# Layer 0 of a two-layer decoder trunk: a finer program order, and one set of tiles for the inverses of two heads

## The chip, the cores and the metric

The kernel runs on 1 core of one Trainium2 chip. The metric is the device time of an execution in microseconds, as the median of the runs. TensorE is called PE here (its weight loads PEld), VectorE DVE, ScalarE ACT, GpSimd POOL, and the queue that issues nearly all DMAs is SyncE's, SP.

## What is computed

Two layers of a decoder on 256 tokens of width 1024, fp32. Layer 0 mixes tokens with Gated DeltaNet (8 heads of 128), layer 1 with sparse attention; both layers also attend to 256 memory tokens with 4 heads, and both end in a gated convolutional feed-forward (width 2816). The part that matters here is Gated DeltaNet for one head, in chunks of the sequence (the kernel uses two chunks of 128 tokens, the reference four of 64; the result is the same):

```
L = where(strict, (k*beta) @ k.T * decay, 0)
T = inverse(I + L)                       # unit lower triangular
u = T @ (v*beta);  w = T @ (k*beta*exp(gc))
a = where(incl, q @ k.T * decay, 0)
for each chunk n:
    v_new = u_n - w_n @ state
    o_n   = (q_n*exp(gc)) @ state + a_n @ v_new
    state = state * g_last + (k_n*exp(gc_last - gc)).T @ v_new
out = rms_norm(o) * silu(z)
```

## The kernel before

**An order made by a planner.** The program is not issued as written. Each call on an engine is recorded as an operation with the tiles that it reads and writes (`Eng`, from line 393), and `Sched.order` then places the operations one by one, as a list scheduler: of the operations that are ready on each engine it takes the one that can start first by the plan's own clock, and among those that could start at once the one that comes first in the program (`op.prio`). It looks at most 1500 operations past the first one not yet placed (`WINDOW`). Buffers of a ring are given out in program order. So the order of the program is an order of priorities. `Sched._cost` gives the duration that the plan assumes for an operation; for a matmul in fp32 with n columns and m output rows it was `(0.009 if m > 32 else -0.028) + 4 * max(m, n) / 2400`, which is 0.0253 us for 32 by 32. Operations made under `PE.group()` or `A.group()` are placed as one. The engines then run what they were given in that order, each in its own.

**Products in halves.** Weights come in chunks of 128x1024 fp32 through SP (`Weights`); ACT rounds a chunk to a high part (`wh`), DVE subtracts for the low part (`wl`), and PE does three products for each block of 128 rows (`proj`: high by high, high by low, low by high, of 256 columns). Tiles of such products are called `pj` (projections of layer 0 and 1) and `pf` (memory keys and values); other PSUM tiles are `mx`.

**Layer 0.** `gdn_pair(p)` is a generator for two heads; `next` runs it to its next `yield`. Before, it has three parts: (A) for both heads, projections of q, k, v, the short convolution, transposes, L (`LL`) and the masked q k product (`AT`); (B) the inverse of I + L for both heads; (C) the projection of z for both, and for both heads the two chunks of state, output and norm. Part B writes LL to DRAM (`scl`) and reads back its 16x16 diagonal blocks, one on each partition (`Lb`); DVE and POOL invert these in 15 steps of two operations (`tm`, `DD`; the planner chooses the engine of each); the result goes to DRAM (`scd`) and comes back laid out by rows (`cd`). Then the blocks are merged on PE: from 16 to 32 rows on the four 32-row quarters of the array (`quads`), from 32 to 64, and from 64 to 128, in two products each (`LL` by the inverse, then the inverse by that), with copies by ACT and DVE between them. Before, these merges run for each head in tiles of its own: `D32` (four buffers), `X`, two PSUM tiles for each step, and the inverse itself in one of four fixed tiles `full`.

The program order of layer 0 was: the memory keys of heads 1 to 3; then by the string `dd0dddddd01021321323`, where `d` is the decay of one head (a DMA, two selects on POOL, four exponentials on ACT) and a digit is the next part of that pair; then the memory values, then the four memory queries with their attention, then `out_proj`. Behind it come the memory keys and values of layer 1 and the feed-forward.

Of the kernel before, what the change touches and what calls it, by code (L numbers as in the profile page):

```python
# [19 lines left out]
P = 128  # L20
# [372 lines left out]
class Eng:  # L393
# [6 lines left out]
    def __getattr__(self, m):  # L400
        def call(*a, **kw):
            op = self._g or Op(self._e)
            op.calls.append((m, a, kw))
            op.name = op.name or m
            args = list(a) + list(kw.values())
            also_out = kw.pop("also_out", ())
            for t in kw.pop("also_in", ()):
                op.reads.add(t)
            outs = ([kw["out"]] if "out" in kw else [a[0]]) + list(also_out)
            if "accum_out" in kw:  # L410
                outs.append(kw["accum_out"])
            for x in args + list(also_out):
                if isinstance(x, (Vt, Ap)):
                    t = x.t if isinstance(x, Ap) else x
                    if t.base is None and t.cls == "whole":
                        continue
                    (op.writes if any(x is o for o in outs) else op.reads).add(t)
            c = self._cost(m, a, kw, outs[0], self._e)
            kw.pop("runs", None)
            op.cost += c  # L420
            if self._o:
                op.alt = {e: (op.alt or {}).get(e, 0.0) + self._cost(m, a, kw, outs[0], e) for e in self._o}
            op.dma = m == "dma_start"
            if m == "activation" and a[2] in (AF.Exp, AF.Silu):
                op.table = a[2]
            if self._g is None:
                self._s.add(op)
            return op
        return call

    def _cost(self, m, a, kw, out, e):
# [6 lines left out]
        if e == "tensor":  # L438
            n = math.prod(out.shape[1:])
            rhs = a[2]  # L440
            if m == "transpose":
                return 0.11
            dt = (rhs.t if isinstance(rhs, Ap) else rhs).dt
            m = out.shape[0]
            if dt == F32R:
                return max(0.013 + 2 * m / 2400, 0.01 + n / 2290)
            return (0.009 if m > 32 else -0.028) + 4 * max(m, n) / 2400
        if e == "vector":
            if m == "reciprocal":
                return 0.06 + 0.0065 * n  # L450
# [29 lines left out]
class Weights:  # L480
# [24 lines left out]
    def block(self, b, n=1):  # L505
# [3 lines left out]
        hi, lo = self.ready[c]  # L509
        return hi[:, r * P:(r + n) * P], lo[:, r * P:(r + n) * P]  # L510


CLASSES = {"q": 12, "d": 37, "k": 57, "s": 43, "ps": 8}

# [15 lines left out]
def body(ctx, tc, xT, memT, vecs, consts, rows, relb, w_few, w_in0, w_out0, w_up0, w_dn0, w_in1, w_out1, w_up1, w_dn1,  # L530
# [37 lines left out]
    def mx():  # L568
        return sc.tile("ps", [P, 512], F32, "mx", 6)
# [165 lines left out]
        kTm[layer, h] = K("kTm", 2 * MH)  # L735
        evac(ps, rm, kTm[layer, h])

    def mem_v(layer, ws, xs, rc):
        for p in range(MH // 2):
            ps = proj_t(ws, (MH + 2 * p) * KD, xs, "pf")  # L740
            for t in range(2):
                v = K("vm", 2 * MH)
                A.mul(v, ps[t], rc[:, t:t + 1])
                vm[layer, p, t] = v

    def mem_attn(layer, h, qmT, rcs=None):
        pss = mx()
# [228 lines left out]
            A.activation(g2[:, t], g2[:, t], AF.Exp, bias=gc[:, t, h:h + 1], scale=-1.0)  # L976
        decays.append((g1, g2))

    full = [fixed([P, 3, P], f"full{i}") for i in range(4)]
    for t in full:  # L980
        PO.memset(t, 0.0)

    def gdn_pair(p):
# [3 lines left out]
        for e, h in enumerate(hd):  # L987
# [47 lines left out]
                V.scalar_tensor_tensor(LL[e][:, t], pgm[:, t * S:t * S + P], sr[:, t:t + 1], g2[:, t], op0=OP.mult, op1=OP.mult)  # L1035
            for t in range(2):
                V.scalar_tensor_tensor(AT[e][:, t], pgm[:, t * S + P:(t + 1) * S], rr[:, t:t + 1], g1[:, t], op0=OP.mult, op1=OP.mult)

        yield

        sl = sc.tile("scl", [4 * US], F32, "scl", 2)
        for e in range(2):
# [9 lines left out]
        for k in range(IB - 1):  # L1052
# [11 lines left out]
        SY.dma_start(cd.rearrange("p w u i -> p (w u) i"),  # L1064
                    sd.raw(lambda r: bass.AP(tensor=r.tensor, offset=r.offset, ap=[[IB, P], [NB * IB * IB, 8], [1, IB]]),
                           [P, 8, IB]), runs=8 * P)

        bd = cst[:, C_BD - C_TRI:C_BD + 2 - C_TRI][:, None, :, None].to_broadcast([P, 2, 2, IB])
        quads = [slice(u, u + 32) for u in range(0, P, 32)]
        for e in range(2):  # L1070
            D = DX[e] = K("D32", 4, shape=(P, 2, 2, 32))
            for w in range(2):
                V.tensor_tensor(out=D[:, w].rearrange("p t (c i) -> p t c i", c=2),
                                in0=cd[:, w, 2 * e:2 * e + 2][:, :, None, :].to_broadcast([P, 2, 2, IB]), in1=bd, op=OP.mult)
            p1 = mx()
            with PE.group():
                for u in quads:
                    for t in range(2):
                        mm(p1[u, t * 32:(t + 1) * 32], LL[e][u, t, u], D[u, 1, t], start=True, stop=True)
            X = K("X", 3, shape=(P, 2, 32))  # L1080
            V.tensor_tensor(out=X, in0=two(p1[:, :64]), in1=D[:, 1], op=OP.add)
            p2 = mx()
            with PE.group():
                for u in quads:
                    for t in range(2):
                        mm(p2[u, t * 32:(t + 1) * 32], X[u, t], D[u, 0, t], start=True, stop=True)
                        mm(p2[u, 64 + t * 32:96 + t * 32], D[u, 0, t], X[u, t], start=True, stop=True)
            V.scalar_tensor_tensor(D.rearrange("p w t i -> p (w t i)"), D.rearrange("p w t i -> p (w t i)"), 2.0, p2[:, :P],
                                   op0=OP.mult, op1=OP.subtract)

        for e in range(2):
            D, F = DX[e], full[hd[e] % 4]
            for u in quads:
                A.copy(F[u, :2, u], D[u, 1])
            for u in quads[:2]:
                A.copy(F[u, 2].rearrange("p (t k) -> p t k", t=2)[:, :, u], D[u, 0])
            p1 = mx()
            with PE.group():
                for E, O in (quads[:2], quads[2:]):
                    for t in range(2):  # L1100
                        mm(p1[E, t * 32:(t + 1) * 32], LL[e][O, t, E], D[O, 1, t], start=True, stop=True)
            X = K("X", 3, shape=(P, 2, 32))
            with A.group():
                for E in quads[::2]:
                    A.copy(X[E], two(p1[E, :64]))
            p2 = mx()
            with PE.group():
                for E, O in (quads[:2], quads[2:]):
                    for t in range(2):
                        mm(p2[E, t * 32:(t + 1) * 32], D[E, 0, t], X[E, t], start=True, stop=True)  # L1110
                for t in range(2):
                    E, O = quads[:2]
                    mm(p2[O, t * 32:(t + 1) * 32], X[E, t], D[E, 0, t], start=True, stop=True)
            with A.group():
                for E, O in (quads[:2], quads[2:]):
                    A.mul(F[E, :2, O], two(p2[E, :64]), -1.0)
                E, O = quads[:2]
                A.mul(F[O, 2].rearrange("p (t k) -> p t k", t=2)[:, :, E], two(p2[O, :64]), -1.0)
        for e in range(2):
            F = DX[e] = full[hd[e] % 4]  # L1120
            E, O = slice(0, 64), slice(64, P)
            p1 = mx()
            with PE.group():
                for t in range(2):
                    mm(p1[E, t * 64:(t + 1) * 64], LL[e][O, t, E], F[O, t, O], start=True, stop=True)
            X = K("X", 3, shape=(64, 2, 64))
            A.copy(X, two(p1[E, :P]))
            p2 = mx()
            with PE.group():
                for t in range(2):  # L1130
                    mm(p2[E, t * 64:(t + 1) * 64], F[E, 2, t * 64:(t + 1) * 64], X[:, t], start=True, stop=True)
            A.mul(F[E, :2, O], two(p2[E, :P]), -1.0)

        yield

# [1 line left out]
        for e, h in enumerate(hd):  # L1137
            ps = proj(w0, (h * 4 + 3) * KD, hs)
            zs[e] = K("zs", 4)
            silu(zs[e], ps, ps, fastz)  # L1140
        for e, h in enumerate(hd):
            pu = mx()
            mm(pu[:, :P], DX[e][:, 0], bv[e][:, 0], start=True, stop=True)
# [36 lines left out]
            y = K("oz", 1)  # L1180
            V.scalar_tensor_tensor(y, pot[:, :S], (vecb if fastz else gnw)[:, 0:1], zs[e], op0=OP.mult, op1=OP.mult)
            mix[h] = hilo(y, "mix", 12, True)

    classes["scl"] = classes["scd"] = 2
    classes["gsc"] = 1
    pools["scl"] = pools["scd"] = pools["gsc"] = pools["dram"]
    for h in range(1, MH):
        mem_k(0, h, wm0, *ms0[:2])
    prs = [gdn_pair(p) for p in range(H // 2)]
    dh = 0  # L1190
    for ch in "dd0dddddd01021321323":
        if ch == "d":
            decay(dh)
            dh += 1
        else:
            next(prs[int(ch)], None)
    mem_v(0, wm0, ms0[0], ms0[2])
    b0 = 32 * KD
    for h in range(MH):
        ps = proj(w0, b0 + h * KD, hs)  # L1200
        q = K("qm", 2)
        A.copy(q, ps)
        mix[H + h] = mem_attn(0, h, q)
    out_proj(w_out0, mix[H:] + mix[:H])
    mts = []
    for k in range(0, KD, 2):
# [5 lines left out]
    mem_v(1, wm1, ms1[0], ms1[2])  # L1212
    hs, rs = normed(V_NFFN)
    ffn(0, w_up0, w_dn0, rs, hs)

# [335 lines left out]
```

## Time and profile before

| | before |
|---|---|
| runs | 809.37, 806.08, 806.21 us, median 806.21 |
| profiled execution | 809.9 us, of which its span is 808.1 us |
| instructions | 15329 |
| busy: PE, PEld | 787.2 us (97%), 714.6 us (88%) |
| busy: DVE, ACT, POOL | 640.6 (79%), 518.7 (64%), 142.0 us (18%) |
| mean granted clock of TensorE | 0.989 |

The span goes from the first to the last instruction. "Busy" is the time in which at least one instruction of the engine is in work. Matmuls overlap, so PE can count as busy throughout and still pass few products; the number of instructions in a stretch (xcount) shows that. Nearly every instruction has the line L389, where the planner issues; so groups are told apart by the names of their tiles, written out<-in.

### The profile page before, as it was taken

What the parts mean: (1) busy time and instruction counts of PE and PEld (TensorE: products, weight loads), DVE (VectorE), ACT (ScalarE), POOL (GpSimd) and SP (SyncE); (2) the same over time, 40 slices, a digit from 0 to 9 for tenths busy, and PEclk for the clock granted to TensorE, in tenths of its full rate; (3) what the DMA queues carried; (4) which work ended last, traced back from release to release, by engine and by line L of the source; (5) the groups of instructions that cost most, each with busy time, mean ns of one, the idle gap of its engine ahead of it and who ended that gap; (6) DMA issues with size and microseconds to landing.
All of it is one profiled execution on the core that took longest, in us unless ns stands there. A gap on an engine that the chain in (4) does not pass through costs nothing.

```text
span 808.1 us, 15329 instructions
## 1 busy us (share of the span) xinstructions
PE 787.2 (97%) x5633; PEld 714.6 (88%) x5633; DVE 640.6 (79%) x1360; ACT 518.7 (64%) x1154; POOL 142.0 (18%) x223
## 2 busy tenths in 40 slices
PE   5999999999999999999999999999999999999995
PEld 5999989999898888888888899999888888888884
DVE  6988958677659898989866687887698989897662
ACT  7579656868764666666543476799646767675340
POOL 1053603352011021221100130000011121212000
PEclk9999979999999999999999999999999999999998
DMA  8575623543415666666656698421365656566641
GB/s 307 216 239 172 180 73 119 170 119 117 130 37 179 207 179 197 184 181 191 192 180 193 191 293 280 151 80 54 108 198 167 200 170 204 177 197 182 196 131 52
DMA packets 52918, 137.22 MB, mean 170 GB/s; under 512 B 11571, under 2 KB 17900, under 8 KB 52716
## 3 DMA queue, kind: packets, MB, share of 16 engines
q1 hardware_dynamic: 52844, 136.26, 55.1%
q8 instruction: 44, 0.72, 0.4%
q14 instruction: 30, 0.25, 0.1%
HBM read 133.86 MB, written 3.95 MB: 171 GB/s over the span
## 4 chain that ended last, share of the span: by engine, by line
PE 90%; DMA 3%; ACT 3%; DVE 2%; issue 1%; SPq 0%; POOL 0%; POOLq 0%; ACTq 0%; DVEq 0%
PE mx L389 66%; PE pj L389 19%; PE pf L389 5%; DMA wr<-in_w_in 1%; ACT full L389 1%; DMA wr<-in_cw 1%; DVE wl L389 1%; ACT wh L389 1%; DMA mt<-in_memT 1%; SPq L389 0%; ACT X L389 0%; POOL rs L389 0%; DVE ln L389 0%; DVE cy L389 0%; POOLq L1546 0%
## 5 line engine op out<-in xcount | busy, mean ns | idle before, releaser
L389 DVE TENSOR_TENSOR wl<-wr,wh 128x1024 fp32r<-128x1024 f32 x224 | 278.4, 1248 | 42.5 <-ACT wh L389 41.6
L389 ACT CAST wh<-wr 128x1024 fp32r<-128x1024 f32 x224 | 232.9, 1046 | 25.7 <-PE mx L389 13.7
L389 PE MATMUL mx<-x,wh 128*128 128x512 f32 x704 | 249.3, 400 | 0.0
L389 PE MATMUL mx<-x,wl 128*128 128x256 f32 x704 | 197.9, 281 | 0.0
L389 PE MATMUL pj<-x,wh 128*128 128x256 f32 x896 | 172.6, 291 | 0.0
L389 PEld LDWEIGHTS mx<-x,wh 128*128 128x128 f32 x704 | 132.4, 188 | 32.7
L389 PEld LDWEIGHTS pj<-x,wh 128*128 128x128 f32 x896 | 139.4, 191 | 2.0 <-issue 0.6
L389 PEld LDWEIGHTS mx<-x,wl 128*128 128x128 f32 x704 | 133.2, 189 | 0.0
L389 PE MATMUL pj<-x,wl 128*128 128x256 f32 x448 | 126.7, 283 | 0.0
L389 PE MATMUL mx<-g,wh 128*128 128x512 f32 x352 | 124.5, 399 | 0.0
L389 PE MATMUL mx<-g,wl 128*128 128x256 f32 x352 | 98.9, 281 | 0.0
L389 PEld LDWEIGHTS pj<-x,wl 128*128 128x128 f32 x448 | 85.5, 191 | 0.0
L389 POOL TENSOR_TENSOR fs<-fs,rs 128x256 f32<-128x256 f32 x44 | 49.7, 1130 | 197.4 <-ACT fs L389 191.6
L389 PEld LDWEIGHTS mx<-g,wh 128*128 128x128 f32 x352 | 66.2, 188 | 16.4
L389 PE MATMUL mx<-mix,wh 128*128 128x512 f32 x192 | 68.3, 401 | 0.0
L389 PEld LDWEIGHTS mx<-g,wl 128*128 128x128 f32 x352 | 66.6, 189 | 0.0
L389 PE MATMUL mx<-mix,wl 128*128 128x256 f32 x192 | 53.6, 279 | 0.0
L389 DVE TENSOR_TENSOR xall<-xall,mx 128x256 f32<-128x256 f32 x64 | 26.8, 419 | 31.8 <-PE mx L389 30.7
L389 ACT COPY half<-mx 128x256 f32<-128x256 f32 x88 | 32.4, 368 | 28.2 <-PE mx L389 26.9
L389 DVE SCALAR_TENSOR_TENSOR fy<-fgr,vecb,fy 128x255 f32<-128x255 f32 x88 | 42.0, 478 | 6.8 <-ACT fy L389 6.8
L389 ACT ACTIVATE x<-xall,vec 128x256 fp32r<-128x256 f32 x24 | 12.2, 510 | 54.7 <-DVE xall L389 54.7
L389 POOL TENSOR_TENSOR sq<-xall 128x256 f32<-128x256 f32 x7 | 9.7, 1386 | 197.5 <-DVE xall L389 197.5
(306 smaller groups left out, 1343.8 us busy)
## 6 DMA issues: line engine op xcount, KB each, us to landing
wr<-in_w_up SPq DMA_DIRECT2D x88, 512.0 KB, 4.4
wr<-in_w_in SPq DMA_DIRECT2D x60, 512.0 KB, 4.4
wr<-in_w_dn SPq DMA_DIRECT2D x44, 512.0 KB, 4.2
wr<-in_w_out SPq DMA_DIRECT2D x24, 512.0 KB, 3.6
mr<-in_w_mem SPq DMA_DIRECT2D x32, 256.0 KB, 4.6
wr<-in_cw SPq DMA_DIRECT2D x8, 512.0 KB, 4.9
mt<-in_memT SPq DMA_DIRECT2D x8, 256.0 KB, 5.0
sk<-skr SPq DMA_DIRECT2D x1, 1536.0 KB, 7.8
```

The source lines that it names most:

```text
L389: i = getattr(getattr(nc, self.eng), m)(*[fix(x) for x in a], **{k: fix(v) for k, v in kw.items()})
```

## The change

`ORDER` takes the place of the string and of the loops around it: 45 letters. `d` is a decay as before, `k` a memory key head (1 to 3), `v` half of the memory values, `q` a memory query head with its attention, and a digit the next part of that pair, of which there are now seven: head A's projections up to AT, head B's, the inverse up to `cd`, the merges, z, head A's state, head B's state. The merges of both heads share their tiles: one `D32`, one `X` and one PSUM tile for a step of both heads, `full` holds two heads in each of two buffers, and each PE group holds the products of both heads and both chunks, with the four quarters as the innermost loop. The plan's charges change in two places: a matmul of at most 32 by 32 counts 0.014 us, and the first of an operation, if its stationary operand is at most 64 by 64, 0.15 us more.

```
-            return (0.009 if m > 32 else -0.028) + 4 * max(m, n) / 2400
+            k = a[1].shape[0]
+            if max(k, m) <= 32:
+                return 0.014
...
+            return 0.009 + 4 * max(m, n) / 2400
...
+            if m == "matmul" and not op.cost and max(a[1].shape) <= 64:
+                c += 0.15
...
+ORDER = "ddk0k0ddddd1010dk01110223032121v322323vqq3q3q"
...
-    full = [fixed([P, 3, P], f"full{i}") for i in range(4)]
+    full = [fixed([P, 2, 3, P], f"full{i}") for i in range(2)]
...
+        et = [(e, t, slice((2 * e + t) * 32, (2 * e + t + 1) * 32)) for e in range(2) for t in range(2)]
-            D = DX[e] = K("D32", 4, shape=(P, 2, 2, 32))
-            for w in range(2):
-                V.tensor_tensor(out=D[:, w].rearrange("p t (c i) -> p t c i", c=2),
-                                in0=cd[:, w, 2 * e:2 * e + 2][:, :, None, :].to_broadcast([P, 2, 2, IB]), in1=bd, op=OP.mult)
+        D = K("D32", 2, shape=(P, 2, 4, 32))
+        V.tensor_tensor(out=D.rearrange("p w u (c i) -> p (w u) c i", c=2),
+                        in0=cd.rearrange("p w u i -> p (w u) i")[:, :, None, :].to_broadcast([P, 8, 2, IB]), in1=bd, op=OP.mult)
...
-                for u in quads:
-                    for t in range(2):
-                        mm(p1[u, t * 32:(t + 1) * 32], LL[e][u, t, u], D[u, 1, t], start=True, stop=True)
+            for e, t, c in et:
+                for u in quads:
+                    mm(p1[u, c], LL[e][u, t, u], D[u, 1, 2 * e + t], start=True, stop=True)
...
-                for u in quads:
-                    for t in range(2):
-                        mm(p2[u, t * 32:(t + 1) * 32], X[u, t], D[u, 0, t], start=True, stop=True)
-                        mm(p2[u, 64 + t * 32:96 + t * 32], D[u, 0, t], X[u, t], start=True, stop=True)
+            for e, t, c in et:
+                for u in quads:
+                    mm(p2[u, c], X[u, 2 * e + t], D[u, 0, 2 * e + t], start=True, stop=True)
+                for u in quads:
+                    mm(p2[u, P + c.start:P + c.stop], D[u, 0, 2 * e + t], X[u, 2 * e + t], start=True, stop=True)
...
-            for u in quads:
-                A.copy(F[u, :2, u], D[u, 1])
+        for u in quads:
+            A.copy(up(u, u), D[u, 1].rearrange("p (e t) k -> p e t k", e=2))
...
+            for e, t, c in et:
+                for E, O in (quads[:2], quads[2:]):
+                    mm(p1[E, c], LL[e][O, t, E], D[O, 1, 2 * e + t], start=True, stop=True)
...
+            for e, t, c in et:
+                mm(p1[E, 2 * c.start:2 * c.stop], LL[e][O, t, E], F[O, e, t, O], start=True, stop=True)
...
-    for h in range(1, MH):
-        mem_k(0, h, wm0, *ms0[:2])
-    for ch in "dd0dddddd01021321323":
...
+    rest = {"d": iter(range(H)), "k": iter(range(1, MH)), "v": iter(range(MH // 2)), "q": iter(range(MH))}
+    for ch in ORDER:
+        if ch.isdigit():
+            next(prs[int(ch)], None)
+        elif ch == "d":
+            decay(next(rest[ch]))
+        elif ch == "k":
+            mem_k(0, next(rest[ch]), wm0, *ms0[:2])
+        elif ch == "v":
+            mem_v(0, next(rest[ch]), wm0, ms0[0], ms0[2])
+        else:
+            mem_head(next(rest[ch]))
```

## Rows read from the trace of the kernel before

**Rows 1.** The page: busy time and share by engine; granted clock in 40 slices.
```profile
PE 787.2 (97%) x5633; PEld 714.6 (88%) x5633; DVE 640.6 (79%) x1360; ACT 518.7 (64%) x1154; POOL 142.0 (18%) x223
...
PEclk9999979999999999999999999999999999999998
```

**Rows 2.** The page: the chain that ended last, shares of the span by engine.
```profile
PE 90%; DMA 3%; ACT 3%; DVE 2%; issue 1%; SPq 0%; POOL 0%; POOLq 0%; ACTq 0%; DVEq 0%
```

**Rows 3.** Stretches: busy us (xcount) of PE, PEld, DVE, ACT, POOL; clock, DMA share, GB/s.
```profile
100.00:110.00 10.00, 8.73 (x173) 7.61 (x173) 8.02 (x26) 8.26 (x30) 0.49 (x2) 0.91 0.57 168
110.00:120.00 10.00, 10.00 (x58) 9.32 (x58) 3.59 (x13) 4.42 (x15) 0.59 (x2) 0.58 0.00 0
120.00:130.00 10.00, 10.00 (x89) 10.00 (x88) 8.36 (x27) 8.16 (x21) 3.47 (x7) 1.00 0.42 115
```

**Rows 4.** Timeline of PE, pair 0's inverse, with the idle time before it.
```profile
106.44 0.44 PE L389 MATMUL mx<-X,D 32*32 32x32 f32 x5 [0.72 <-ACT X L389]
```

**Rows 5.** Timeline of SP's queue: start us, us, what it issues.
```profile
101.29 2.05 SPq L389 DMA_DIRECT2D mr<-in_w_mem  x4
123.47 0.33 SPq L389 DMA_DIRECT2D scd<-DD  x1
```

**Rows 6.** Waits from 100 to 120 us: total us, times, longest.
```profile
DVE kTm L389 <- PE pf L389: 3.5, 1, 3.5
```

**Rows 7.** Timeline of PE, pair 2's inverse: start us, us, instruction.
```profile
178.22 0.28 PE L389 MATMUL pj<-x,wl 128*128 128x256 f32 x1
178.43 0.49 PE L389 MATMUL mx<-D,LL 32*32 32x32 f32 x32
178.85 0.50 PE L389 MATMUL pj<-x,wh 128*128 128x256 f32 x2
179.19 0.28 PE L389 MATMUL pj<-x,wl 128*128 128x256 f32 x1
179.40 0.24 PE L389 MATMUL mx<-D,X 32*32 32x32 f32 x2
...
180.83 0.50 PE L389 MATMUL pj<-x,wh 128*128 128x256 f32 x2
...
181.38 0.32 PE L389 MATMUL mx<-D,LL 32*32 32x32 f32 x8
181.63 0.44 PE L389 MATMUL mx<-ident,o 128*128 128x128 f32 x2
...
182.71 0.40 PE L389 MATMUL pj<-x,wh 128*128 128x256 f32 x2
182.95 0.28 PE L389 MATMUL pj<-x,wl 128*128 128x256 f32 x1
...
183.51 0.23 PE L389 MATMUL mx<-X,D 32*32 32x32 f32 x2
...
183.78 0.50 PE L389 MATMUL pj<-x,wh 128*128 128x256 f32 x2
...
185.49 0.44 PE L389 MATMUL mx<-full,LL 64*64 64x64 f32 x4
185.86 0.51 PE L389 MATMUL pj<-x,wh 128*128 128x256 f32 x2
...
188.12 0.68 PE L389 MATMUL mx<-X,full 64*64 64x64 f32 x8
188.72 0.50 PE L389 MATMUL pj<-x,wh 128*128 128x256 f32 x2
```

**Rows 8.** Timeline of PE: first and last run of small products in layer 0.
```profile
101.95 0.49 PE L389 MATMUL mx<-D,LL 32*32 32x32 f32 x32
...
218.81 0.44 PE L389 MATMUL mx<-X,full 64*64 64x64 f32 x4
```

**Rows 9.** Groups, 0 to 240 us: busy us, mean ns, idle before.
```profile
L389 ACT COPY full<-D 32x64 f32<-32x64 f32 x48 | 11.6, 242 | 7.3 <-DVE D L389 6.8
...
L389 DVE TENSOR_TENSOR D<-cd,cst 128x64 f32<-128x64 f32 x16 | 2.8, 220 | 0.0
```

More of the change, by code (lines that the diff above doesn't have):

```diff
@@ L736, in mem_k, with mem_v @@
         evac(ps, rm, kTm[layer, h])
-    def mem_v(layer, ws, xs, rc):
-        for p in range(MH // 2):
-            ps = proj_t(ws, (MH + 2 * p) * KD, xs, "pf")
-            for t in range(2):
-                v = K("vm", 2 * MH)
-                A.mul(v, ps[t], rc[:, t:t + 1])
-                vm[layer, p, t] = v
+    def mem_v(layer, p, ws, xs, rc):
+        ps = proj_t(ws, (MH + 2 * p) * KD, xs, "pf")
+        for t in range(2):
+            v = K("vm", 2 * MH)
+            A.mul(v, ps[t], rc[:, t:t + 1])
+            vm[layer, p, t] = v
     def mem_attn(layer, h, qmT, rcs=None):
@@ L1037, in gdn_pair @@
                 V.scalar_tensor_tensor(AT[e][:, t], pgm[:, t * S + P:(t + 1) * S], rr[:, t:t + 1], g1[:, t], op0=OP.mult, op1=OP.mult)
-        yield
+            yield
         sl = sc.tile("scl", [4 * US], F32, "scl", 2)
@@ L1066, in gdn_pair @@
                            [P, 8, IB]), runs=8 * P)
-        bd = cst[:, C_BD - C_TRI:C_BD + 2 - C_TRI][:, None, :, None].to_broadcast([P, 2, 2, IB])
+        yield
+        bd = cst[:, C_BD - C_TRI:C_BD + 2 - C_TRI][:, None, :, None].to_broadcast([P, 8, 2, IB])
         quads = [slice(u, u + 32) for u in range(0, P, 32)]
-        for e in range(2):
-            D = DX[e] = K("D32", 4, shape=(P, 2, 2, 32))
-            for w in range(2):
-                V.tensor_tensor(out=D[:, w].rearrange("p t (c i) -> p t c i", c=2),
-                                in0=cd[:, w, 2 * e:2 * e + 2][:, :, None, :].to_broadcast([P, 2, 2, IB]), in1=bd, op=OP.mult)
-            p1 = mx()
-            with PE.group():
-                for u in quads:
-                    for t in range(2):
-                        mm(p1[u, t * 32:(t + 1) * 32], LL[e][u, t, u], D[u, 1, t], start=True, stop=True)
[L1080 to L1083, printed above, removed]
-                for u in quads:
-                    for t in range(2):
-                        mm(p2[u, t * 32:(t + 1) * 32], X[u, t], D[u, 0, t], start=True, stop=True)
-                        mm(p2[u, 64 + t * 32:96 + t * 32], D[u, 0, t], X[u, t], start=True, stop=True)
-            V.scalar_tensor_tensor(D.rearrange("p w t i -> p (w t i)"), D.rearrange("p w t i -> p (w t i)"), 2.0, p2[:, :P],
-                                   op0=OP.mult, op1=OP.subtract)
@@ L1091, in gdn_pair @@
-        for e in range(2):
-            D, F = DX[e], full[hd[e] % 4]
-            for u in quads:
-                A.copy(F[u, :2, u], D[u, 1])
[L1095 to L1132, printed above, removed]
+        et = [(e, t, slice((2 * e + t) * 32, (2 * e + t + 1) * 32)) for e in range(2) for t in range(2)]
@@ new lines, in gdn_pair @@
+        four = lambda ap: two(ap, 4)
+        D = K("D32", 2, shape=(P, 2, 4, 32))
+        V.tensor_tensor(out=D.rearrange("p w u (c i) -> p (w u) c i", c=2),
+                        in0=cd.rearrange("p w u i -> p (w u) i")[:, :, None, :].to_broadcast([P, 8, 2, IB]), in1=bd, op=OP.mult)
+        p1 = mx()
+        with PE.group():
+            for e, t, c in et:
+                for u in quads:
+                    mm(p1[u, c], LL[e][u, t, u], D[u, 1, 2 * e + t], start=True, stop=True)
+        X = K("X", 3, shape=(P, 4, 32))
@@ new lines, in gdn_pair @@
+        V.tensor_tensor(out=X, in0=four(p1[:, :P]), in1=D[:, 1], op=OP.add)
+        p2 = mx()
+        with PE.group():
+            for e, t, c in et:
[3 more added lines that the diff above has]
+                    mm(p2[u, P + c.start:P + c.stop], D[u, 0, 2 * e + t], X[u, 2 * e + t], start=True, stop=True)
+        V.scalar_tensor_tensor(D.rearrange("p w u i -> p (w u i)"), D.rearrange("p w u i -> p (w u i)"), 2.0, p2[:, :S],
+                               op0=OP.mult, op1=OP.subtract)
@@ new lines, in gdn_pair @@
+        F = full[p % 2]
+        up = lambda r, c: F[r, :, :2, c]
+        low = lambda r, c: F[r, :, 2].rearrange("p e (t k) -> p e t k", t=2)[:, :, :, c]
+        heads = lambda ap: ap.rearrange("p (e t k) -> p e t k", e=2, t=2)
+        for u in quads:
+            A.copy(up(u, u), D[u, 1].rearrange("p (e t) k -> p e t k", e=2))
+        for u in quads[:2]:
+            A.copy(low(u, u), D[u, 0].rearrange("p (e t) k -> p e t k", e=2))
+        p1 = mx()
+        with PE.group():
+            for e, t, c in et:
+                for E, O in (quads[:2], quads[2:]):
+                    mm(p1[E, c], LL[e][O, t, E], D[O, 1, 2 * e + t], start=True, stop=True)
@@ new lines, in gdn_pair @@
+        X = K("X", 3, shape=(P, 4, 32))
+        with A.group():
+            for E in quads[::2]:
+                A.copy(X[E], four(p1[E, :P]))
+        p2 = mx()
+        with PE.group():
+            for e, t, c in et:
+                for E in quads[::2]:
+                    mm(p2[E, c], D[E, 0, 2 * e + t], X[E, 2 * e + t], start=True, stop=True)
+                E, O = quads[:2]
+                mm(p2[O, c], X[E, 2 * e + t], D[E, 0, 2 * e + t], start=True, stop=True)
+        with A.group():
+            for E, O in (quads[:2], quads[2:]):
+                A.mul(up(E, O), heads(p2[E, :P]), -1.0)
+            E, O = quads[:2]
+            A.mul(low(O, E), heads(p2[O, :P]), -1.0)
@@ new lines, in gdn_pair @@
+        E, O = slice(0, 64), slice(64, P)
+        p1 = mx()
+        with PE.group():
+            for e, t, c in et:
+                mm(p1[E, 2 * c.start:2 * c.stop], LL[e][O, t, E], F[O, e, t, O], start=True, stop=True)
+        X = K("X", 3, shape=(64, 4, 64))
+        A.copy(X, four(p1[E, :S]))
+        p2 = mx()
+        with PE.group():
+            for e, t, c in et:
+                mm(p2[E, 2 * c.start:2 * c.stop], F[E, e, 2, t * 64:(t + 1) * 64], X[:, 2 * e + t], start=True, stop=True)
@@ L1134, in gdn_pair @@
+        A.mul(up(E, O), heads(p2[E, :S]), -1.0)
+        for e in range(2):
+            DX[e] = F[:, e]
         yield
@@ L1140, in gdn_pair @@
             silu(zs[e], ps, ps, fastz)
+        yield
         for e, h in enumerate(hd):
@@ L1182, in gdn_pair @@
             mix[h] = hilo(y, "mix", 12, True)
+            yield
     classes["scl"] = classes["scd"] = 2
@@ L1186, in body, with mem_head @@
     pools["scl"] = pools["scd"] = pools["gsc"] = pools["dram"]
-    for h in range(1, MH):
-        mem_k(0, h, wm0, *ms0[:2])
-    prs = [gdn_pair(p) for p in range(H // 2)]
-    dh = 0
-    for ch in "dd0dddddd01021321323":
[L1192 to L1200, printed above, removed]
+    def mem_head(h):
+        ps = proj(w0, (32 + h) * KD, hs)
         q = K("qm", 2)
@@ L1203, in body @@
         mix[H + h] = mem_attn(0, h, q)
+    prs = [gdn_pair(p) for p in range(H // 2)]
+    rest = {"d": iter(range(H)), "k": iter(range(1, MH)), "v": iter(range(MH // 2)), "q": iter(range(MH))}
[10 more added lines that the diff above has]
+            mem_head(next(rest[ch]))
     out_proj(w_out0, mix[H:] + mix[:H])
@@ L1211, in body @@
         mem_k(1, h, wm1, *ms1[:2])
-    mem_v(1, wm1, ms1[0], ms1[2])
+    for p in range(MH // 2):
+        mem_v(1, p, wm1, ms1[0], ms1[2])
     hs, rs = normed(V_NFFN)
```

## The prediction

> **What bounds the kernel now.** I read the busy times and the slices of the page first, then the chain of waits, then layer 0 in stretches of 10 us, then TensorE (PE) instruction by instruction. PE is busy 97% of the span and is 90% of the chain that ended last [rows 1, 2]; VectorE (DVE) at 79% and ScalarE (ACT) at 64% are not the bound over the whole. So a change pays by what PE no longer does, or no longer waits for. "Busy" hides much, though: a stretch can be 10 us busy out of 10 and yet pass 58 matmuls where its neighbour passes 89 [rows 3]. That is the one bad place of layer 0: between 100 and 120 us the granted clock averages 0.91 and 0.58, that is, 18% and 84% of the time at the lower of its two levels (1.2 instead of 2.4 GHz). Before it fell, PE stood still for small things, as 0.72 us for ACT to copy X [rows 4]. The SyncE queue (SP) tells why nothing better was at hand: after four loads issued from 101.29 us it issues nothing until 123.47 us, where it writes DD out [rows 5]. SP works in order, so every weight load that the plan put behind that write waited 20 us for the 16x16 inversions of pair 1. These are 30 small steps passed between DVE and GpSimd (POOL), and DVE, in order too, stood 3.5 us before a kTm that PE had not finished [rows 6]. With no new weights PE had only memory products left.
>
> **The price of small products now.** A matmul instruction in fp32 leaves two records, so "x32" is 16 products. Dense products start 0.12 us apart (two from 182.71 to 182.95). A run of 32- or 64-wide products costs more than its length: the last dense product ahead of it takes 0.21 us (178.22 to 178.43), 0.09 extra, and the first two behind it take 0.34 instead of 0.24 us (178.85 to 179.19, against 182.71 to 182.95), 0.10 extra: 0.19 us for each run [rows 7]. There are 33 runs in layer 0; the first and the last stand in [rows 8]. In pair 2, where nothing waits, the run lengths to the next dense product are: first products of both heads 0.42 us (16 products; 0.30 without the 0.12 to the next start, 19 ns each); second products 1.43 us (32, 45 ns each); then one run for each head of 0.25 (4 products), of 0.27 (6) and of 0.37 us (two 64-wide); and 0.60 us for the last four 64-wide together [rows 7].
>
> **The change, part by part.** (1) *Turn through the quarters.* The number of products stays (76 for a pair). Before, a second product stands four deep on one 32-row quarter before the next quarter comes; after, four consecutive ones go to four quarters. The first products stand two deep and already come at 19 ns, the second ones four deep at 45, so depth is what costs. I take 19 ns for the second ones too: 32 x 0.019 + 0.12 = 0.73 instead of 1.43 us, 0.70 saved, 2.8 us for four pairs. Bounds: 45 ns stays (0), or a quarter of it, 11 ns (3.8 us). The first products may gain up to 16 x 8 ns = 0.13 a pair (0.5 in all); I take 0.
> The Trainium skill, "TensorEngine Tiling (Array Packing)", section "Gotcha 1: PSUM Pressure", speaks against this: row tiles, it says, can't access one PSUM bank at the same time, and the four quarters here write one PSUM tile. By that rule the turn would gain nothing (the rival of serial quarters, below). The 19 ns against 45 ns above speak for overlap within one tile. "TensorE: Matmul & The Clock Gate", section "Wait — 56ns, not 53.3ns?", has starts never closer than about 25 ns; by it, with 25 ns a product, the saving would be 2.0 instead of 2.8 us, as an estimate; the 19 ns measured here are below it.
> (2) *Two heads in one group.* Each later step keeps its products and saves one 0.12 us to the next dense start: 0.12 at the 4-product step, 0.12 at the 6-product step, 0.12 at the first 64-wide one, and about 0.1 at the last (pair 2 runs it together already). 0.46 a pair, 1.8 us in all; 0 if a joint step waits as long as it saves. All products of a 64-wide step sit on one quarter of the array before and after, so nothing is won there by order.
> (3) *Fewer runs.* Six groups for a pair instead of up to twelve: 33 runs become 24, 9 x 0.19 = 1.7 us. Bounds: 0, if the joint groups stand behind one another less often than the single ones did, and 1.7.
> So PE does 2.8 + 1.8 + 1.7 = 6.3 us less, bounds 0 and 7.8 (3.8 + 0.5 + 1.8 + 1.7).
> (4) *Fewer evacuations.* ACT's 48 copies of 0.242 us into full become 24 twice as wide, DVE's 16 multiplications of 0.22 us for D become 4 [rows 9]. At most half of 11.6 us of ACT goes, at least nothing. This lies beside PE; cost and gain of it I put at nothing, hidden by dense products as now. If that cover is gone, each joint step shows its wait: 0.72 us a piece [rows 4]. A joint step starts when both heads are ready; behind its first product on PE's queue stand dense ones. The inversions of both heads came from one DMA before too, so no wait is added at the head of the chain. I add two such waits, 1.5 us; bounds -1 (the start gains) and +7 (a new stretch like 100 to 120).
> (5) *The order.* 45 parts instead of 20. Moved are: memory keys of heads 1 to 3 with their loads on SP, the last decay (its load on SP, its two selects on POOL), the z projections, each head's state steps, and the memory values and queries, which now stand between the last states. The inversion of pair 1 comes ahead of pair 2's projections, where it was behind them, so its five small DMAs stand before pair 2's weight loads in priority. The planner still issues whatever can start first within 1500 operations, so this shifts priorities and not a fixed list.
> (6) *The charges.* The plan had 0.0253 us for a 32-wide product whatever its depth, 0.81 for a step that took 1.43 plus 0.19 [rows 7]. New are 0.014, and 0.15 to enter. The plan runs less ahead of the chip behind each inversion, and what DVE, POOL and SP queue behind a planned time is late by less.
> With (5) and (6) I expect the stretch from 100 to 120 us to close. Its price: clock (0.09 + 0.42) x 10 = 5.1 us, and 10.0 - 8.73 = 1.3 us of idle PE [rows 3], 6.4 together. Bounds: 0 to 6.4.
>
> **The sum.** Against the profiled execution (809.9 us, its span of 808.1 and 1.8 around it): 809.9 - 6.3 - 6.4 + 1.5 = 798.7. The median of the timed runs is 806.21, 3.7 lower, and one of them is at 809.37. I take it that most of the lower clock is missing in the lower runs, which no row shows. Then only 6.4 - 3.7 = 2.7 us of the stretch are in the median: 806.2 - 6.3 - 2.7 + 1.5 = 798.7 again. I say 799.
>
> **Rivals.**
> *Serial quarters:* the turn gains nothing, for instance since all four quarters write one PSUM tile, and the new order leaves the stretch as it is. 806.2 - 1.8 - 1.7 = 802.7. For it: the 45 ns have not been seen to shrink. Against it: 19 ns at half the depth.
> *Order without effect:* the planner's choice hardly moves and the stretch stays, but the products shrink: 806.2 - 6.3 = 799.9. The time can't tell this from the forecast, the clock row can.
> *More holes (the other side):* SP again stands behind a DD that DVE and POOL finish late, now in more than one of the four inversions, since each is planned closer to other work. Price 6.4 us a hole. One, as now, gives 799.9; two give 806.3, no gain; three give 806.2 - 6.3 + 2 x 6.4 = 812.7. It decides from the third on. For it: one of four inversions does it today. Against it: three don't, and the charges are nearer to the chip.
> *More than forecast:* quarters at 11 ns (3.8 + 0.5 instead of 2.8), no added waits, and 1 us less at the start: 799 - 1.5 - 1.5 - 1 = 795.
>
> **Chances.** Forecast 0.43, with a range of its own from 795 to 803; order without effect 0.07; serial quarters 0.24; more holes 0.14; more than forecast 0.12. The range of 792 to 809 takes in the bounds of the small products (7.8 and 0) and part of the holes. A measurement of this kernel tells about 0.5%, 4.0 us, from no change, so faster means below 802.2 and slower above 810.2. Faster: 0.85 x 0.50 + 0.12 + 0.3 x 0.24 = 0.62; slower: most of the holes and little else, 0.12; the same 0.26.
>
> **What would show it.** (1) right: the 32 second products of a pair take about 0.7 us from the first start to the next dense one; wrong: 1.4. (2, 3): 24 runs or fewer, and no joint step ending later than two single ones. (4): no row of PE waiting over 0.7 us for ACT's X or full, more than twice. (5, 6): no stretch of layer 0 with a granted clock below 0.9, and no 20 us in which SP issues nothing; the first products of out_proj come some 10 us earlier than now. If they do and the total doesn't follow, the later stages have given it back, which I hold for unlikely, as their order in the program is the same. The forecast is wrong if layer 0 shows a second hole, or if the second products stay at 45 ns.

## The result, and the profile after

The changed kernel takes 797.04 us in the median against 807.51 us of the kernel before, a ratio of 0.9872 with a 95% interval from 0.9844 to 0.99: faster, as forecast, and 2 us from the 799 us that were forecast. Its profiled execution took 797.3 us (span 795.5), 12.6 us less than the 809.9 us that the sum was made against. Of these, 11.0 lie ahead of layer 0's down-projection, whose first product started at 394.81 us and now starts at 383.84; 1.9 come from layer 1's mixer, which no step had, and 0.3 are lost behind it.

The page after: busy time, granted clock in 40 slices, and the chain by engine. It answers to [rows 1, 2].

```profile
PE 775.5 (97%) x5633; PEld 704.5 (89%) x5633; DVE 639.4 (80%) x1341; ACT 509.4 (64%) x1102; POOL 147.0 (18%) x220
...
PEclk9999999999999999999999999999999999999998
...
PE 86%; issue 4%; ACT 3%; DVE 3%; DMA 2%; POOL 1%; SPq 0%; POOLq 0%; DVEq 0%
```

PE is still busy 97% of a span that is 12.6 us shorter; its busy time is 11.7 us shorter. The 7 in the slices of the clock is gone. The stretches of [rows 3], after:

```profile
20.00:30.00 10.00, 9.86 (x71) 9.26 (x70) 9.43 (x22) 6.57 (x15) 1.55 (x1) 0.84 0.87 334
...
100.00:110.00 10.00, 9.56 (x172) 8.56 (x171) 6.99 (x22) 8.17 (x24) 2.64 (x6) 1.00 0.39 117
110.00:120.00 10.00, 10.00 (x87) 9.94 (x86) 7.82 (x27) 5.89 (x18) 1.45 (x4) 1.00 0.34 79
```

From 110 to 120 us PE passes 87 products where it passed 58, at the full clock. The 0.84 at the start is no new loss. In the first profile of the kernel before, whose record of the clock begins only at 22.8 us, dense products stood at the lower pace until then: three take 0.64 us from start to start (20.38 to 21.02), and 0.36 us right behind (23.12 to 23.48).

```profile
20.38 0.63 PE L389 MATMUL pf<-mem,mh 128*128 128x256 f32 x2
...
21.02 0.63 PE L389 MATMUL pf<-mem,mh 128*128 128x256 f32 x2
...
23.12 0.40 PE L389 MATMUL pf<-mem,mh 128*128 128x256 f32 x2
...
23.48 0.40 PE L389 MATMUL pf<-mem,mh 128*128 128x256 f32 x2
```

In its second profile (next section) the full pace came at 17 us, and the first inverse 2.1 us earlier; the changed kernel had it from 16 us, and lost it again from 19.8 to 23.2 us. So some 2 of the 11.0 us belong to the start of that one execution and not to the change.

The timeline of PE in pair 2's inverse, which answers to [rows 7]: each small run, and the dense product behind it.

```profile
171.19 0.45 PE L389 MATMUL mx<-D,LL 32*32 32x32 f32 x32
171.58 0.50 PE L389 MATMUL pf<-mem,mh 128*128 128x256 f32 x2
...
173.34 0.26 PE L389 MATMUL mx<-D,X 32*32 32x32 f32 x8
...
174.03 0.44 PE L389 MATMUL mx<-ident,o 128*128 128x128 f32 x2
...
175.11 0.44 PE L389 MATMUL mx<-D,LL 32*32 32x32 f32 x16
175.48 0.50 PE L389 MATMUL pj<-x,wh 128*128 128x256 f32 x2
...
177.10 0.22 PE L389 MATMUL mx<-X,D 32*32 32x32 f32 x2
...
177.48 0.50 PE L389 MATMUL pj<-x,wh 128*128 128x256 f32 x2
...
180.53 0.68 PE L389 MATMUL mx<-full,LL 64*64 64x64 f32 x8
181.14 0.66 PE L389 MATMUL mx<-ident,mp 128*128 128x128 f32 x4
...
182.12 0.68 PE L389 MATMUL mx<-X,full 64*64 64x64 f32 x8
182.73 0.50 PE L389 MATMUL pj<-x,wh 128*128 128x256 f32 x2
```

The 32 second products take 0.69 us (173.34 to 174.03) instead of 1.43; the steps behind them 0.37, 0.38, 0.61 and 0.61 us for both heads together. The queue of SP, which answers to [rows 5]:

```profile
101.83 2.31 SPq L389 DMA_DIRECT2D mr<-in_w_mem  x3
114.97 0.33 SPq L389 DMA_DIRECT2D scd<-DD  x1
```

The gap ahead of the write of DD is 10.8 us instead of 20.1. Over layer 0 the small runs are 24 instead of 33 and last 12.1 instead of 19.1 us together (the lengths to the next other product, summed over the timeline).

### The profile page after: what moved, and what is told of

Same layout as the page of the kernel before. It is cut to its first block, busy times and chain, and to the rows that moved or that the text cites. A ratio compares the mean times of both kernels' runs of the same rounds, so it can differ in the third digit from the quotient of the medians.

```text
span 795.5 us, 15212 instructions
## 1 busy us (share of the span) xinstructions
PE 775.5 (97%) x5633; PEld 704.5 (89%) x5633; DVE 639.4 (80%) x1341; ACT 509.4 (64%) x1102; POOL 147.0 (18%) x220
## 4 chain that ended last, share of the span: by engine, by line
PE 86%; issue 4%; ACT 3%; DVE 3%; DMA 2%; POOL 1%; SPq 0%; POOLq 0%; DVEq 0%
PE mx L389 67%; PE pj L389 15%; PE pf L389 4%; DVE wl L389 1%; ACT wh L389 1%; ACT g L389 1%; DMA mr<-in_w_mem 1%; DVE win L389 1%; DMA mt<-in_memT 1%; DMA wr<-in_cw 1%; POOL rr L389 0%; ACT full L389 0%; POOL rs L389 0%; DVE cmpT L389 0%; SPq L389 0%
## 5 line engine op out<-in xcount | busy, mean ns | idle before, releaser
L389 ACT COPY half<-mx 128x256 f32<-128x256 f32 x88 | 32.2, 366 | 20.0 <-PE mx L389 19.4
```

The lines of the kernel that those rows point to most:

```text
L389: i = getattr(getattr(nc, self.eng), m)(*[fix(x) for x in a], **{k: fix(v) for k, v in kw.items()})
```

## The experiments

On the chips of these runs the kernel before spreads from 802 to 812 us, so the table gives, beside each median and its ratio to the kernel before on the same chip, three numbers of the trace: when the down-projection of layer 0 starts, how long the clock was at its lower level between 90 and 250 us, and how long PE stood in the merges of pair 0, the first of the four. (The first of the three also holds when an execution got its full clock, between 11 and 24 us from its start.)

| kernel | median us | ratio (95%) | down-projection, us | low clock, us | PE stood in pair 0, us |
|---|---|---|---|---|---|
| before, first profile | 807.51 | | 394.81 | 10.2 | 1.27 |
| before, again | 807.3 (one run) | | 392.89 | 10.2 | 1.27 |
| changed | 797.04 | 0.9872 (0.9844 to 0.99) | 383.84 | 0 | 0.44 |
| changed, again | 795.6 | 0.9851 (0.9811 to 0.9891) | 383.53 | 0 | 0.44 |
| changed, deep on a quarter | 803.87 | 0.996 (0.9933 to 0.9987) | 389.37 | 0 | 0.44 |
| changed, old charges | 801.04 | 0.9921 (0.989 to 0.9951) | 388.18 | 3.4 | 1.55 |
| changed, old order | 803.2 | 0.9949 (0.9929 to 0.997) | 386.23 | 0 | 0.89 |
| merges alone | 800.7 | 0.9907 (0.989 to 0.9924) | 387.08 | 0 | 1.11 |
| turn alone | 808.43 | 0.9993 (0.9975 to 1.0011) | 390.91 | 13.7 | 2.02 |
| order alone | 815.88 | 1.009 (1.0056 to 1.0124) | 401.58 | 13.7 | 0.69 |
| charges alone | 811.24 | 1.0046 (1.002 to 1.0072) | 398.24 | 13.7 | 1.72 |
| order and charges | 808.5 | 1.001 (0.9995 to 1.0025) | 396.47 | 6.8 | 0.35 |
| DD written by POOL | 811.54 | 1.0042 (1.0012 to 1.0072) | 398.05 | 13.7 | 1.09 |
| DD written and read by POOL | 820.15 | 1.0142 (1.0122 to 1.0161) | 404.98 | 13.7 | 3.12 |

**The changed kernel again**, nothing edited.

> The changed kernel once more, as the measure for the three beside it: 797 us, 0.987 of the kernel before. If the kernel before again has runs at 806 and at 809 us, the higher ones should be those with the lower mean clock.

Measured 795.6 us, 0.9851. What told its profiles apart (span 792.1 against 795.5 us) was not the clock but the feed-forward of layer 1; the last section has it.

**Deep on a quarter.** Only the loops of the first two merge steps change:

```
-            for e, t, c in et:
-                for u in quads:
+            for u in quads:
+                for e, t, c in et:
                     mm(p1[u, c], LL[e][u, t, u], D[u, 1, 2 * e + t], start=True, stop=True)
...
+            for u in quads:
+                for e, t, c in et:
+                    mm(p2[u, c], X[u, 2 * e + t], D[u, 0, 2 * e + t], start=True, stop=True)
+                    mm(p2[u, P + c.start:P + c.stop], D[u, 0, 2 * e + t], X[u, 2 * e + t], start=True, stop=True)
```

> The changed kernel with the two first merge steps in the old sequence: all products of one 32-row quarter in a row, then the next quarter. The plan charges both sequences alike, so the order of everything else stays. If depth on a quarter sets the price: a pair's 32 second products go from 0.68 us back to some 1.4 us, +2.8 us over the changed kernel, 800 us. If the quarters don't overlap in a useful way, or other work covers it: under 0.5 us, 797 us.

Measured 803.87 us; the down-projection starts 5.5 us later than in the changed kernel, with the same order of all else. PE's timeline in pair 2, first and second products with what comes behind:

```profile
173.53 0.89 PE L389 MATMUL mx<-D,LL 32*32 32x32 f32 x32
174.35 0.50 PE L389 MATMUL pf<-mem,mh 128*128 128x256 f32 x2
...
176.12 0.24 PE L389 MATMUL mx<-D,X 32*32 32x32 f32 x2
...
177.96 0.44 PE L389 MATMUL mx<-ident,o 128*128 128x128 f32 x2
```

0.82 and 1.84 us instead of 0.39 and 0.69: with two heads a quarter holds four and eight products in a row, so both steps cost more than in the changed kernel, 1.58 us a pair, 6.3 in all. All of it arrives: from the first product of the first inverse to the down-projection it is 290.99 us here (98.38 to 389.37) and 284.63 us in the changed kernel (99.21 to 383.84), with the same 0.44 us of standing. I had expected 1.4 us for the second step, the price at depth four. Without the 0.12 us to the next start, a product costs 18 ns in turn, 19 two deep, 41 four deep ([rows 7]: 1.43 less 0.12 us, by 32), 44 four deep in the first products here, and 54 eight deep (1.72 / 32): depth sets the price.

**Old charges** in the changed kernel (the two charges as they were before), and **old order** in it (`ORDER = "kkkdd00dddddd00110002211332211133222333vvqqqq"`, the parts of before in the new letters).

> The changed kernel with the charges of before (0.0253 us for a 32-wide product, nothing to enter). If the charges are what closes the stretch in which SP stands behind a late inverse: the stretch comes back, 3 to 6 us, 800 to 803 us, with SP issuing nothing for 15 us or more. If the order string does it: within 1 us of the changed kernel.

> The changed kernel with the parts of layer 0 in the program order of before, written in the new letters. If the order closes the bad stretch: it comes back, +3 to +6 us over the changed kernel, 800 to 803 us. If the smaller products are the whole gain: within 1 us of the changed kernel, 797 to 798 us.

Both cost: the down-projection comes 4.3 and 2.4 us later, the medians are 5 and 8 us above the changed kernel on that chip. But only the old charges bring the lower clock back, for 3.4 us, and SP's gaps ahead of DD are 12.9 and 13.2 us, not 20. With the old order PE stands instead, at the last 64-wide step and behind it:

```profile
107.40 0.67 PE L389 MATMUL mx<-X,full 64*64 64x64 f32 x8 [0.89 <-ACT X L389]
...
109.12 0.71 PE L389 MATMUL mx<-bv,full 128*128 128x128 f32 x4 [1.04 <-ACT full L389]
```

So taking either one out costs. That doesn't make each worth something by itself: these two kernels are the merges with the order alone (0.9921) and with the charges alone (0.9949), and the merges without either, below, stand at 0.9907. Only both together go below that.

**The kernel before again**, for its trace.

> The kernel before once more, for its trace. If the lower clock at 108 to 118 us is what tells its runs at 809 us from those at 806 us, it is missing in a run near 806 us and the feed-forward stages last the same. The rival since the last runs: the feed-forward's 512-column products start 236.7 us/1000 apart in some executions and 230.0 in others, 2 to 7 us in all, and this sets the spread; then the clock dip stands again whatever the time.

It ran at 807.3 us, 2.6 below the first profile, and the dip is there all the same (windows of it, columns as in [rows 3]):

```profile
100.00:110.00 10.00, 8.73 (x170) 7.40 (x158) 6.78 (x23) 7.55 (x29) 0.50 (x2) 0.81 0.39 116
110.00:120.00 10.00, 10.00 (x62) 9.66 (x63) 4.09 (x18) 4.36 (x16) 0.85 (x3) 0.68 0.00 0
```

10.2 us at the lower level in both. Of 72 more runs of the kernel before, on three chips, 59 have a mean granted clock of 0.988 to 0.990, as the two profiles have, and none is above 0.993; without the 10.2 us it would be 0.006 more, about 0.995. The assumption that the lower runs mostly lack the dip falls. Here 2.1 us of the difference lie ahead of the first inverse (its first product at 99.8 instead of 101.95 us), where the full pace came 5 us earlier.

**Order alone, charges alone, both.** The inverses of before; new `yield`s and `ORDER`, or the two charges, or all of it.

> The kernel before with the new order of 45 parts alone: inverses a head at a time as before, charges as before. If the order alone closes the bad stretch: some 5 us under the kernel before, 0.994. If it needs the smaller products or the charges: within 2 us of the kernel before, with the gap of SP ahead of the write of DD still near 20 us.

> The kernel before with the new charges alone. They now say 0.014 us for products that take 0.045 here, so the plan is not nearer to the chip in the second products; the 0.15 to enter is nearer. By the theory that a plan near the chip closes the stretch: 0 to 3 us faster. By the theory that the stretch hangs on the order of the pairs: within 1 us of the kernel before, gap of SP near 20 us.

> Order and charges together on the inverses of before, the merges left out. If the two close the bad stretch as the forecast's steps (5) and (6) have it: down-projection at 388 to 390 us. If they work only on merged inverses, as each alone did worse than nothing (401.6 and 398.2 us): 397 us or more, and slower than the kernel before by 0.3% or more.

None is faster: 1.009, 1.0046 and 1.001. All three have the lower clock behind pair 0's merges, the first two a second time near 215 us. Order alone shows two stretches at the lower clock, as the forecast's rival of more holes has it:

```profile
110.00:120.00 10.00, 9.29 (x53) 8.73 (x53) 5.35 (x19) 6.50 (x20) 2.00 (x4) 0.66 0.02 5
210.00:220.00 10.00, 8.37 (x57) 7.10 (x56) 3.92 (x11) 7.93 (x31) 1.68 (x6) 0.67 0.01 2
```

Its SP gap ahead of DD is 15.4 us, and it is the only one of its kind: at the second stretch SP's gap (19.4 us, to 221.7 us) ends with a load for layer 1, and PE stands 1.6 us for ACT in pair 3's merges. So the holes came, but the second for another reason than the rival's. In the profiles, order and charges don't close the stretch on the old inverses, alone or together. (With both, the profile is one of the longer runs, 811.05 us at a mean clock of 0.992. Four of the twelve have 0.996 or 0.997, which suggests that they lack the stretch, though no trace shows it; at 806.3 to 807.4 us they are hardly below the kernel before, 807.97.)

**Turn alone.** The kernel before, loops over `t` outside and the quarters inside; all engines keep their order.

```
-                for u in quads:
-                    for t in range(2):
+                for t in range(2):
+                    for u in quads:
                         mm(p1[u, t * 32:(t + 1) * 32], LL[e][u, t, u], D[u, 1, t], start=True, stop=True)
```

> The kernel before with the turn through the quarters alone, a head at a time; every engine's order stays as it was. A head's 16 second products go from about 0.72 us to 0.38: 0.34 x 8 = 2.7 us. If PE time is what counts: total 2 to 3 us less, ratio 0.9965. If the gain turns into waits, as in the stretch behind the late write of DD: under 1 us.

The second products of pair 2 go from 1.43 to 0.68 us (176.59 to 177.27), 3.0 us in four pairs, and the median doesn't move: 0.9993 (0.9975 to 1.0011). In pair 0 the saving is given back at once, at the next wait, which was 0.72 us in [rows 4]:

```profile
104.28 0.44 PE L389 MATMUL mx<-X,D 32*32 32x32 f32 x5 [1.48 <-ACT X L389]
```

0.76 us more, as much as the product step saved. And a second stretch of 3.4 us at the lower clock stands at 214.8 us. Over the four pairs PE stands 3.1 us, against 1.8 in the second profile of the kernel before; with 1.7 us for the lower clock (half of 3.4, an estimate) that is about the 3.0 us that the turn saved. (Its feed-forward of layer 0 ran at the quicker of the two paces of the last section, so the down-projection's start flatters it; the feed-forward itself starts at 268.11 us, against 267.87 in the second profile of the kernel before.)

**Merges alone.** The merged, turned inverses with the order and charges of before.

> The merged inverses alone: program order and charges of before. Time to the first down-projection of layer 0 (first product that reads g), which was 394.8 and 392.9 us in the kernel before, 383.8 and 383.5 in the changed one, 386.2 with merges and charges, 388.2 with merges and order: if the merges carry the gain and order and charges add to it: 387 to 390 us, total about 0.993. If merges need one of the other two: 392 us or more.

Measured 800.7 us, 0.9907, down-projection at 387.08 us: the first of the two cases. Two thirds of the gain are here, without a low clock behind pair 0:

```profile
100.00:110.00 10.00, 9.04 (x193) 8.03 (x192) 7.82 (x22) 8.82 (x27) 1.71 (x5) 1.00 0.72 228
110.00:120.00 10.00, 9.71 (x84) 9.38 (x84) 7.68 (x30) 6.79 (x22) 1.19 (x3) 1.00 0.03 7
```

**DD through POOL's queue.** The kernel before with `PO.dma_start` for the write of DD, and in a second one for its read-back as well.

> The kernel before with one DMA of each inverse, the write of DD to DRAM, issued by POOL instead of SP, so that no weight load stands behind it. If SP's wait for DD is what starves PE from 100 to 120 us: the 20 us gap of SP goes, the clock there stays at 2.4 GHz, and the time falls by 4 to 6 us, ratio 0.993 to 0.995. If PE is starved by its own chain of small steps and not by late weights: gap gone, but PE waits and a low clock stay there, time within 2 us.

> The kernel before with the write of DD and its read-back both issued by POOL, since with the write alone the read-back on SP took over the gap (20.3 us). If SP's block starves PE of weights: no SP gap over 9 us before 200 us, the clock from 100 to 120 us stays up, down-projection at 389 us or earlier. If PE is starved by the inverse's own chain, the gap goes and the low clock stays, 393 us or later.

With the write alone, SP's gap stayed (20.3 us) in front of the read-back, so it decided nothing. With both off SP, the gap is still there, now between two plain weight loads:

```profile
102.05 1.84 SPq L389 DMA_DIRECT2D mr<-in_w_mem  x4
104.86 21.77 SPq L389 DMA_DIRECT2D wr<-in_w_in  x2
```

The second of these loads comes 21.1 us behind the first. No write of DD stands ahead of it; the profile puts SP's wait down to DVE, at a step of the states:

```profile
SPq L389 <- DVE o L389: 21.2, 1, 21.2
```

The low clock lasts 10.2 us as before, and PE stands in its own merges:

```profile
105.11 0.22 PE L389 MATMUL mx<-D,X 32*32 32x32 f32 x2 [0.89 <-DVE X L389]
...
108.13 0.49 PE L389 MATMUL mx<-X,D 32*32 32x32 f32 x5 [0.73 <-ACT X L389]
110.09 0.69 PE L389 MATMUL mx<-full,LL 64*64 64x64 f32 x4 [1.30 <-ACT full L389]
```

So taking DD off SP takes away neither the gap nor the low clock. As a test of late weights this is not clean, since the loads are late here too. The kernel before settles it itself. From 98 to 118 us PE waits for nothing but ACT, and the weights of its next projection lie ready for some 18 us:

```profile
PE mx L389 <- ACT X L389: 0.7, 1, 0.7
PE mx L389 <- ACT full L389: 0.5, 1, 0.5
...
99.74 1.22 DVE L389 TENSOR_TENSOR wl<-wr,wh 128x1024 fp32r<-128x1024 f32 x1
...
118.83 0.48 PE L389 MATMUL pj<-x,wh 128*128 128x256 f32 x2
```

SP issues nothing from 103.34 to 123.47 us and DVE makes no other low part of a chunk until 124.09, so the projection that starts at 118.83 us runs on weights that were there by 101 us. PE passed memory products ahead of it because they came first in its order. So the reading that late weights starve PE is wrong. Part of SP's gap, on the contrary, is a late PE: DVE, which makes most of DD, stood 3.5 us [rows 6] and 1.5 us for products of PE within it. (Both kernels are also slower, 1.0042 and 1.0142; how much of that is POOL's queue and how much the other order that the planner made isn't separated.)

## Why the prediction was right, and where its reasons failed

**Sum and sign** were right: 809.9 - 6.3 - 6.4 + 1.5 = 798.7 forecast, 797.3 in the profile, and the rows that were to show it did: 0.69 us for the second products (0.73 forecast), 24 runs, no stretch of layer 0 with a granted clock under 0.9 but the one at the start, no 20 us of SP without an issue, PE's wait for ACT in pair 0 once and 0.44 us. One sign can't be read: out_proj's first product comes 28.6 us earlier (206.08 instead of 234.67), not some 10, because its products are now spread over 49 us instead of 35, with other work between.

That the sum came out within 2 us is in part luck. Its 12.6 us in the profiles hold 1.9 us of layer 1's mixer, which no step had, and some 2 us of the start. Against the second profile of the kernel before, the down-projection comes 9.1 us earlier (383.84 instead of 392.89). The two parts as measured below, 6.4 us of small products and 6.4 us of the stretch, are 12.8. So 2 to 4 us of them were given back elsewhere in layer 0; in the sum the 1.5 us of new waits happened to stand for that, but those waits did not come, and where it went wasn't traced.

**(1) to (3), PE does less:** forecast 6.3 us. In pair 2, undisturbed in both, the runs went from 4.23 to 3.05 us, 4.7 for four pairs, and nine runs fewer at 0.19 us are 1.7: 6.4. The joint steps saved 0.41 us a pair instead of 0.46: the last 64-wide step saved nothing (0.61 against 0.60 us). The 45 ns of the prediction still held the 0.12 us that its 19 ns had left out; like for like it is 41, and the term, which went by 1.43 us, doesn't hang on it. What failed is the silent step that PE's saving is time saved. On the old inverses the turn saves 3.0 us of PE and none of the time; on the merged ones, where PE stands 0.44 us with either loop, all 6.3 us of the turn arrive. The merges are a chain of PE, DVE and ACT. Where PE stands in it already, a shorter PE step lengthens the wait for ACT, as from 0.72 to 1.48 us in pair 0.

**(4), evacuations at nothing:** wrong, as far as the runs tell. ACT's part of the merges (copies into full and X, the negated ones) went from 23.9 to 15.2 us, summed from the groups, and PE's standing in pair 0 from 1.27 to 0.44. The turn alone gives nothing, turn and joint tiles together 7.3 us (merges alone), of which 5.1 are the price of the 10.2 us at the lower clock that are gone (half of them, an estimate). The difference must come from joining, that is from fewer, wider evacuations, fewer runs and the order that the planner then makes. These three were not separated. That it is a lucky order alone is unlikely: the four orders seen with merged and turned inverses give 0.9851 to 0.9949, and all seen with the old ones 0.9993 to 1.0142.

**(5) and (6), the stretch:** it closed, 6.4 us as priced (5.1 for the clock, and PE stands 1.3 us less), but not for the reason given. The step "with no new weights PE had only memory products left" was wrong: the weights lay ready. In the profiles order and charges close nothing without the merges; the merges close it without them. What the low clock goes with is what PE does in pair 0's merges: in the kernel before, 27 dense products stand among the small ones and PE stands 1.27 us; in the changed kernel 42, and 0.44 us. All seven kernels with the old inverses have a low clock there, 6.8 us or more; of the five with merged ones, one, for 3.4 us. The standing by itself doesn't sort them: order and charges stood 0.35 us and lost the clock, the merges alone stood 1.11 us and kept it. The dense products among the merges do, 42 in each kernel that kept the clock and fewer in each that lost it, but that they are the cause isn't shown, and what would suffice isn't known from this. Order and charges together are worth 3 to 5 us on top of the merges, and each alone nothing; 1.2 us of that is less standing of PE in the four merges (0.44 instead of 1.63 us), and the rest wasn't traced.

**The median against the profile:** the step that put 3.7 us of the dip outside the median was wrong; the dip is in the run at 807.3 us too. By this sum the median was to fall by 7.5 us, from 806.2; it fell by 10.5. The result was near all the same because the median of before moved up by 1.3 us with one more run, which is luck.

**Rivals:** serial quarters is refuted by the 0.69 us. With it falls, for quarters that write different partitions of one PSUM tile, the rule of the Trainium skill, "TensorEngine Tiling (Array Packing)", section "Gotcha 1: PSUM Pressure", as the forecast applied it; the measurement decides. More holes is seen for the order alone, with one SP gap ahead of a DD and not two. That the order changes little is refuted by the same kernel, whose down-projection starts 7 to 9 us later than before. More than forecast was half met: a product costs 18 ns and not 11, but no wait was added.

## What to carry to other kernels

Where small products are chained with copies by other engines, measure whether PE waits behind them before pricing a faster product: a saving ahead of a wait can be lost, and joining two chains into half as many, wider links can pay where the faster product alone does not. A queue that issues nothing for 20 us needn't starve anyone: look what the consumer waits for, and whether its next weights already lie there, before calling the queue the cause. Two changes to a planner's input can each cost alone and pay together, so test them both ways. Here products in a row on one 32-row quarter cost more the more of them there were (18 ns in turn, 54 eight deep), so turn through the quarters in the innermost loop, above all when more products are put into one group.

## What the runs showed of the hardware that was not expected

The feed-forward's products have two paces, at a full granted clock and with the same program. Windows of 60 us in layer 1's up-projection, first of the changed kernel's profile, then of its second one:

```profile
640.00:700.00 60.00, 60.00 (x341) 52.05 (x340) 54.46 (x96) 40.57 (x75) 11.96 (x11) 1.00 0.63 185
```

```profile
640.00:700.00 60.00, 60.00 (x348) 52.91 (x347) 55.84 (x99) 41.59 (x77) 12.25 (x11) 1.00 0.62 193
```

341 against 348 products. A 512-column product started 0.2367 us before the next in one and 0.2300 in the other, from about 600 us to the end. This alone is 3.4 us between the two spans, all of it behind 597 us, where the two stood within 0.03 us of each other. The turn alone had the quicker pace in layer 0's feed-forward and the slower in layer 1's. What sets the pace wasn't found; it is part of the spread of equal kernels here, and a reason to read a change of a few us from the trace ahead of such a stage.
